# Half-precision parts in the projections of layer A of a two-layer streaming encoder

## The chip, the cores and the metric

The kernel runs on one core of a Trainium2 chip. The metric is the device time of one execution in microseconds (us); the figure for a kernel is the median of its runs. The profile is of one further execution. Its engines are PE (TensorE; its weight loads are shown as PEld), DVE (VectorE), ACT (ScalarE), POOL (GpSimd) and SP (SyncE, which issues all DMAs of this kernel).

## What is computed

There are 2048 prompt tokens and 64 sample tokens of width 1024, and two layers of gated attention with 16 heads of 64. Both layers have the form `x + W_out(attention(RMSNorm(x)) * silu(gate))`; queries, keys, values and gate come from one input projection, and queries and keys are normalised by head.

- Layer A: 16 query heads over 2 key/value heads, a window of a chunk of 64 tokens and the two chunks before, a sink for each head and a bias by relative position.
- Layer B: 16 heads with keys and values of their own, a window of nine chunks, and another bias.

```python
def project(x, norm_g, w_in, q_g, k_g, n_heads, n_kv):
    h = rms_norm(x, norm_g)
    p = h @ w_in
    wq = n_heads * HEAD_DIM
    wkv = n_kv * HEAD_DIM
    q, k, v, gate = jnp.split(p, [wq, wq + wkv, wq + 2 * wkv], axis=-1)
    ...
```

`rms_norm` divides each token by the root of its mean square and multiplies each column by a gain `g`. The kernel puts that gain into the weights.

## The kernel before

**Products of two parts.** All products are of single precision. Each operand is split into a high and a low part, and a product is three matmuls: high by high, high by low, low by high (`project`, lines 796 to 798; the sample unit has both parts of its 64 tokens side by side and needs two, lines 791 and 792). In layer A the parts are of the type fp32r, four bytes wide; in layer B they are float16. Float16 has a narrow range, so layer B brings its operands into range first: weights are multiplied by a power of two found from their largest value, tokens by their row's norm, and the product is multiplied by one constant at its evacuation.

**Units and passes.** Tokens are worked on in units of 256, two tiles of 128, with the 64 sample tokens as a unit of their own. The order is units 0 to 6, the sample, unit 7. Layer A goes over all units four times (passes, `qd` 0 to 3). A pass projects 512 columns, 256 of queries and 256 of gate (four heads); the first pass projects 256 columns of keys and values besides. Then come layer A's output projection, layer B in eight passes over the heads, and its output projection.

**The order of the work.** TensorE's instructions stand in the order in which the program writes them; those of the other engines are placed by a scheduler with a model of the time. A `Filler` holds the projections as generators with costs, and the pipeline of attention items draws on it: attention for tile i runs while the projection is three tiles ahead (`pipeline`). `Filler.step` asks for the next unit's tokens (`prefetch`) when a unit's projection begins, and for the next pass's weights one unit ahead, in passes three and four three units ahead. A `Background` queue holds the splits and evacuations; it is drained in shares between the attention's steps, one or two weight chunks a share, and what a matmul needs is run by force ahead of it (`weights_of`).

**Tokens.** `load_act` loads a unit in four chunks of 128 x 512 into `xraw` (four buffers), casts the high part on ACT (L677), and subtracts on POOL for the low part (L678). The parts are kept in DRAM (`xsa`): units 0 and 1 are split in the first and again in the second pass and stored in the second, the others are split and stored in the first. Later passes load them. `KEEP` holds in which pass a unit is stored. In layer A four loads of 512 KB bring a unit back; in layer B, where the parts are float16, it is two.

**Row norms.** The tokens' factors `rr[0]` come from `row_scales`: it loads the tokens by rows into `xraw`, squares them on ACT with a sum (L772), and raises the mean to -1/2 on POOL (L779). For units 0 and 1 they come from column sums. In layer A the factor of each token is applied when a projection is evacuated (`evacuate`, `evacuate_a`); in layer B `token_rows` spreads the factors over the partitions by a small matmul (L752) and the tokens are multiplied on DVE ahead of the split (L674).

**Weights.** `load_weights` loads chunks of 128 x 512 through three `wraw` buffers. The first set of layer A has twelve chunks (four of keys and values, eight of queries and gate) and later sets have eight. A chunk's high part is made on ACT (L579), its low part on DVE (L582). The loading of a chunk is asked for when the third chunk ahead of it is split.

**Scans.** The scales of layer A's output projection need the largest absolute value of its weights and of the gate's weights. `scan` loads a chunk of 128 x 512 into one buffer and takes a maximum on DVE (L181); `scales_ahead` does so for 16 chunks, every second item from item 20 on, and takes 32 maxima of 128 x 256 from the gate's columns of the split weights (`gate_top`, L261). At items 56 to 58 the scale is worked out (`first_top`, `first_across`, `first_scales`).

**PSUM.** The projections share two banks (`pj`), and attention in layer A has four (`sa`). Line 819 and lines 835 and 836 are evacuations of projections on ACT; line 890 is the multiplication by the head norm on DVE, the last reader of a query/gate bank.

## Time and profile before

| | us |
|---|---|
| median of three runs | 2062.57 |
| lowest, highest | 2062.24, 2062.81 |
| the profiled execution's own time | 2071.44 |
| its span, first to last instruction | 2069.7 |
| granted TensorE clock, mean | 0.992 |

In the profile the projections of layer A lie in these stretches, read from the first and last matmul of 512 columns of each pass: the first from 17.4 to 217.6 us (key/value matmuls start at 6.7), the second from 219.4 to 357.5, the third from 357.8 to 503.2, the fourth from 503.5 to 642.6. The first float16 projection of layer B starts at 841.4.

How to read the rows: a group's row has the line of the program, engine and operation, the tile written and those read, the shape, the count, then busy time and the mean in ns of one, and the engine's idle time just before with what ended it. Matmuls are pipelined and their ends are modelled, so their durations overlap; the distance of their starts tells what one costs. A line can be a helper's. Waits are put down to the releaser that came last.

### The profile page before, as it was taken

What the parts mean: (1) busy time and instruction counts of PE and PEld (TensorE: products, weight loads), DVE (VectorE), ACT (ScalarE), POOL (GpSimd) and SP (SyncE); (2) the same over time, 40 slices, a digit from 0 to 9 for tenths busy, and PEclk for the clock granted to TensorE, in tenths of its full rate; (3) what the DMA queues carried; (4) which work ended last, traced back from release to release, by engine and by line L of the source; (5) the groups of instructions that cost most, each with busy time, mean ns of one, the idle gap of its engine ahead of it and who ended that gap; (6) DMA issues with size and microseconds to landing.
All of it is one profiled execution on the core that took longest, in us unless ns stands there. A gap on an engine that the chain in (4) does not pass through costs nothing.

```text
span 2069.7 us, 40501 instructions
## 1 busy us (share of the span) xinstructions
PE 1975.7 (95%) x12723; PEld 1382.1 (67%) x12723; DVE 1440.7 (70%) x4163; ACT 1438.7 (70%) x3560; POOL 1134.8 (55%) x1529
## 2 busy tenths in 40 slices
PE   7899999999999999989999999999999999999999
PEld 6777777777877888545555555555555555557788
DVE  7666877877778433677667676676767767677673
ACT  6887888777789443377677787786877778687330
POOL 5665565544446323477556575665656656565540
PEclk9999999999999999999999999999999999999999
DMA  8878887998776555698989788897997978698753
GB/s 264 260 210 233 230 215 207 238 243 243 206 187 192 168 177 162 229 235 219 237 177 237 177 201 220 168 253 162 212 211 182 215 167 187 151 189 205 189 158 106
DMA packets 593816, 420.20 MB, mean 203 GB/s; under 512 B 403696, under 2 KB 522880, under 8 KB 593568
## 3 DMA queue, kind: packets, MB, share of 16 engines
q1 hardware_dynamic: 593600, 417.60, 79.9%
q8 instruction: 101, 1.65, 0.3%
q14 instruction: 115, 0.94, 0.1%
HBM read 248.68 MB, written 73.43 MB: 156 GB/s over the span
## 4 chain that ended last, share of the span: by engine, by line
PE 58%; DVE 12%; DMA 10%; ACT 8%; issue 6%; POOL 5%; SPq 1%; POOLq 0%; ACTq 0%; DVEq 0%
PE pj L796 11%; PE pj L798 10%; PE pj L797 10%; PE o L1908 4%; DMA pt<-values 3%; PE sb L1744 2%; PE pj L2164 2%; PE sb L1745 2%; PE pj L2166 2%; PE pj L2165 2%; PE tp L1054 2%; PE pj L2413 2%; PE pj L2417 2%; PE pj L2416 2%; DVE p L1748 1%
## 5 line engine op out<-in xcount | busy, mean ns | idle before, releaser
L796 PE MATMUL pj<-wh,xx 128*128 128x512 f16 (+2 forms) x1648 | 642.9, 390 | 19.8 <-ACT pa L819 9.1
L798 PE MATMUL pj<-wh,xx 128*128 128x512 f16 (+2 forms) x1648 | 624.6, 379 | 0.0
L1801 POOL TENSOR_TENSOR values<-p,values 128x640 f16<-128x640 f32 (+4 forms) x256 | 328.2, 1282 | 206.9 <-ACT values L1800 202.7
L797 PE MATMUL pj<-wh,xx 128*128 128x512 f16 x1024 | 389.9, 381 | 1.3 <-DVE wh L582 1.3
L1760 ACT ACTIVATE p<-p,nm 128x640 f32<-128x640 f32 (+5 forms) x264 | 199.6, 756 | 181.4 <-DVE nm L1753 148.7
L1748 DVE CUSTOM_DVE_ANT_0 p<-sb,BT 128x640 f32<-128x640 f32 (+5 forms) x272 | 196.4, 722 | 148.1 <-PE sb L1745 120.9
L797 PE MATMUL pj<-wl,xx 128*128 128x512 f32 (+1 forms) x624 | 234.8, 376 | 2.3 <-DVE wl L582 2.3
L887 POOL TENSOR_TENSOR f<-f,mhalf 128x4 f32<-128x4 f32 x182 | 188.0, 1033 | 11.7
L798 PEld LDWEIGHTS <-xx 128*128 128x128 f16 x1024 | 100.6, 98 | 123.6 <-issue 3.8
L1561 POOL TENSOR_TENSOR o<-gt,o 128x256 f32<-128x256 f32 (+1 forms) x132 | 106.4, 806 | 139.5 <-ACT p L1391 63.9
L1800 ACT CAST values<-p 128x640 f16<-128x640 f32 (+4 forms) x256 | 168.2, 657 | 12.7 <-DMA pt<-values 6.5
L1391 ACT ACTIVATE p<-p,nm 128x257 f32<-128x257 f32 (+2 forms) x272 | 134.3, 496 | 59.3 <-DVE nm L1380 26.6
L797 PEld LDWEIGHTS <-xx 128*128 128x128 f16 x1024 | 100.6, 98 | 84.2 <-issue 4.9
L796 PEld LDWEIGHTS <-xx 128*128 128x128 f16 x1024 | 100.6, 98 | 82.0 <-issue 1.9
L1908 PEld LDWEIGHTS <-values 128*128 128x128 f16 x1344 | 123.8, 98 | 41.2 <-issue 2.8
L1908 PE MATMUL o<-pt,values 128*128 128x256 f16 (+1 forms) x1344 | 144.7, 256 | 3.6 <-DMA pt<-values 3.6
L796 PEld LDWEIGHTS pj<-wh,xx 128*128 128x128 f32 x624 | 118.6, 190 | 40.3 <-ACT pa L819 11.0
L798 PEld LDWEIGHTS pj<-wh,xx 128*128 128x128 f32 x624 | 118.4, 190 | 23.1
L886 POOL TENSOR_TENSOR f<-f,small 128x4 f32<-128x4 f32 x182 | 38.5, 211 | 172.5 <-DVE f L883 152.7
L797 PEld LDWEIGHTS pj<-wl,xx 128*128 128x128 f32 x624 | 119.1, 191 | 17.6 <-DVE wl L582 3.2
L1556 ACT COPY o<-o 64x256 f32<-64x256 f32 (+1 forms) x264 | 96.1, 364 | 37.8 <-PE o L1908 27.3
L678 POOL TENSOR_TENSOR xx<-xraw,xx 128x512 fp32r<-128x512 f32 (+3 forms) x80 | 97.4, 1233 | 44.3 <-ACT xx L677 44.0
(389 smaller groups left out, 5157.7 us busy)
## 6 DMA issues: line engine op xcount, KB each, us to landing
xx<-xsb SPq DMA_DIRECT2D x112, 512.0 KB, 4.3
xx<-xsa SPq DMA_DIRECT2D x88, 512.0 KB, 5.0
xsa<-xx SPq DMA_DIRECT2D x32, 512.0 KB, 4.2
wl<-in_w_in_b_dram SPq DMA_DIRECT2D x64, 256.0 KB, 4.8
wraw<-in_w_in_b_dram SPq DMA_DIRECT2D x56, 256.0 KB, 3.6
xraw<-in_x_dram SPq DMA_DIRECT2D x40, 256.0 KB, 4.4
xraw<-oga SPq DMA_DIRECT2D x32, 264.0 KB, 3.2
xraw<-ogb SPq DMA_DIRECT2D x32, 264.0 KB, 3.5
```

The costliest lines, as they stand in the source:

```text
L678: nc.gpsimd.tensor_tensor(lo, rv, wide(hi), op=ALU.subtract)
L796: nc.tensor.matmul(ps[:n, :C], xh, wh, start=k == 0, stop=False)
L797: nc.tensor.matmul(ps[:n, :C], xh, wl, start=False, stop=False)
L798: nc.tensor.matmul(ps[:n, :C], xl, wh, start=False, stop=k == KC - 1)
L887: nc.gpsimd.tensor_tensor(fv, fv, mhalf[:n, :H], op=ALU.pow)
L1391: ex = nc.scalar.activation(pv[:n, h % 2, : nk + 1], pv[:n, h % 2, : nk + 1], AF.Exp, scale=-1.0, bias=nm[:n, h : h + 1], accum_out=sm[:n, ...
L1561: nc.gpsimd.tensor_tensor(o1v, gtv, o1v, op=ALU.mult)
L1748: mi = nc.vector.tensor_tensor_reduce(out=p[r, :nk], in0=S[r, o : o + nk], in1=b, op0=ALU.add, op1=ALU.min, scale=1.0, scalar=3e38, accum_ ...
L1760: ex = nc.scalar.activation(p[:n, :nk], p[:n, :nk], AF.Exp, scale=-1.0, bias=it.nm[:n, c : c + 1], accum_out=it.sm[:n, c : c + 1],)
L1800: hi = nc.scalar.copy(two[:, :, 0, :], pv)
L1801: lo = nc.gpsimd.tensor_tensor(two[:, :, 1, :], pv, two[:, :, 0, :], op=ALU.subtract)
L1908: nc.tensor.matmul(it.O[:, h * T + q0 : h * T + q1_], held["VH"][:, kt, h], x, start=kt == kb and not low, stop=kt == tb and low == 1,)
```

## The change

- The first three units of the first pass (`SW = 3`) are projected as before. From the fourth on (`place >= SW`) and in all later passes the projections use float16 parts of tokens that are multiplied by their factor first (`token_rows(unit, 0)`), and weights with a scale (`gsa`); the evacuation multiplies by one constant `C_A(q)`.
- The first pass's weights are therefore split twice: in fp32r for three units, and again in float16. For the second split all twelve chunks are loaded anew, through three raw buffers. Eight are asked for after the last projection of the second unit, four in the third unit after its keys and values, which are now projected for both tiles first. Their scale comes from maxima of the fp32r high parts (`hi_top`, `key_top`), taken between the projections of the second unit's first tile, with a transpose on TensorE in its second tile (`input_across_a`) and a broadcast after it (`input_scales_a`).
- The weights of passes two to four are scanned ahead: 24 scans more, from item -2 on, one for each item up to item 37, where the 16 of the output weights now follow without a pause. `gate_top` is gone; the maxima of whole chunks stand in for it.
- The third unit, too, is split in the first and again in the second pass (`KEEP`), and `xsa` is float16: two transfers of 512 KB for a unit in place of four.
- Of the multiplications by the row factors, those of every second chunk go to POOL, the others to DVE.
- Row norms from the fifth unit on are worked out two units ahead of the one being projected instead of one.
- The second pass's weights are asked for two units ahead, half of them first.

```diff
+SW = 3
+KEEP = [1] * SW + [0] * (NU + 1 - SW)
...
     def scan_source(i):
+        if i >= 100:
+            return w_qg_a[(i - 92) // 8, (i - 100) % 8 // 2, :, i % 2, :]
...
+    def hi_top(w, i, ks, part):
         for k in ks:
             wt, j = w[k]
             r = nc.vector.tensor_reduce(
+                most[:, i + k : i + k + 1], wide(wt.h[:, j, part]), axis=AX.X, op=ALU.max,
                 apply_absolute_value=True,
             )
+            behind(r.ins, bg.anchors.get(r.ins.engine, held["ms"]))
...
+    def input_across_a(q):
+        ps = psum_a("sa", 512, 4)
+        nc.tensor.transpose(ps[0:1, 0:P], top[:, 15 + q : 16 + q], ident)
+        m, e, r = (row[:, i : i + 1] for i in (60, 61, 62))
+        nc.vector.tensor_reduce(m, ps[0:1, 0:P], axis=AX.X, op=ALU.max)
+        nc.vector.tensor_scalar(m, m, 1e-12, 1.0, op0=ALU.max, op1=ALU.mult)
+        powers(m, e, r)
+        times(row[:, 46:47], r, WB_)
+        times(row[:, 47:48], e, 1 / (HB * WB_))
+
+    def input_scales_a(q):
+        ps = psum_a("sa", 512, 4)
+        nc.tensor.matmul(
+            ps[:, 0:2], ones[0:1, 0:1].to_broadcast([1, P]), row[:, 46:48], start=True, stop=True
+        )
+        nc.vector.tensor_copy(scl[:, 10 + q, 0:2], ps[:, 0:2])
+        times(gsa[:, q], gain[:, 0, :], scl[:, 10 + q, 0:1])
+        held["known", q] = True
...
+    xs = [dr.tile([P, 2 * KC * TOK], dt, tag=n, name=n) for n, dt in (("xsa", F16), ("xsb", F16))]
...
+        def place_first(i):
+            tag = ("wx", "ws", "wh")[i // 4]
+            return t(tag, [P, 1024], WN if i >= 8 else 4, F16)
...
                     if rows is not None:
-                        (nc.vector).tensor_tensor(
+                        (nc.gpsimd if cache is xs[0] and c % 2 == 0 else nc.vector).tensor_tensor(
...
+                if half_parts:
+                    assert ("known", qd) in held
+                    rows = None if qd > KEEP[u] else token_rows(unit, 0)
+                    st.x[qd, u] = x = load_act(
+                        x0, u * UT, T, False, T == TS, None, cache, qd > KEEP[u], F16, rows
+                    )
+                else:
+                    st.x[qd, u] = x = load_act(x0, u * UT, T, sums, T == TS, lead)
...
                 if qd not in st.emit:
-                    (st.w[qd],), _, st.emit[qd] = load_weights(0, (w_qg_a[qd], 512))
+                    assert ("known", qd) in held
+                    (st.w[qd],), _, st.emit[qd] = load_weights(1, (w_qg_a[qd], 512), scale=gsa[:, qd])
...
+                    if qd == 0 and place >= SW - 1:
+                        for later in order[place + 2 + (it is not mine[0]) : place + 3 + (it is not mine[0])]:
+                            if later[0] not in held["normed"]:
+                                row_scales(later)
+                                held["normed"].add(later[0])
+                    if qd == 0 and place == SW - 1:
+                        if it is mine[0]:
+                            for it2 in mine:
+                                out = []
+                                c = yield from project(it2.tile, xc, st.wkv, 256, out)
+                                take_kv(it2, out[0])
+                                yield c
+                            st.emit_more(4)
...
+                    if qd == 0 and u == 1:
+                        if it is mine[0]:
+                            key_top(st.wkv)
+                            hi_top(st.w[0], 24, range(8), slice(0, 512))
+                        else:
+                            input_top_a(0)
+                            input_across_a(0)
                     out = []
                     c = yield from project(it.tile, xc, st.w[qd], 512, out)
                     take_qg(it, out[0])
+                    if qd == 0 and u == 1 and it is mine[1]:
+                        input_scales_a(0)
+                        st.halves, _, st.emit_more = load_weights(
+                            1, (w_qg_a[0], 512), (w_kv_a, 256), scale=gsa[:, 0], apart=None
+                        )
+                        st.emit_more(8)
...
-            filler.add(prefetch, weights if place == 0 else None, first if qd == 0 and u == 0 else gen, 3 * (qd > 1))
+            filler.add(prefetch, weights if place == 0 else None, first if qd == 0 and u == 0 else gen, (0, 2, 3, 3)[qd])
...
         def scales_ahead(i):
+            n = i + 2
+            if 0 <= n < 40:
+                scan(100 + n if n < 24 else 60 + n)
+            elif n == 40:
                 scan()
...
+            if i == 42:
                 first_top()
+            elif i == 44:
                 first_across()
+            elif i == 46:
                 first_scales()
```

123 lines of the change are left out of this document (64 added, 59 removed).

## The prediction, made before the result was known

> **What bounds the kernel now.** I read the page first, then a table of windows cut at the passes of layer A, then the waits of TensorE in those windows, then the groups by shape, and last single matmuls in order of time.
>
> ```profile
> span 2069.7 us, 40501 instructions
> PE 1975.7 (95%) x12723; PEld 1382.1 (67%) x12723; DVE 1440.7 (70%) x4163; ACT 1438.7 (70%) x3560; POOL 1134.8 (55%) x1529
> ```
>
> The page says only that TensorE is busy nearly all the time. Whether a faster matmul shortens the kernel has to be read in the stage that is changed. The columns below are the window, its length, then the busy time of PE, PEld, DVE, ACT and POOL, the granted clock, the DMA share and GB/s. The rows are: the first pass around its fourth unit, the rest of the first pass, and passes two, three and four.
>
> ```profile
> 37.00:90.00 53.00, 44.21 (x267) 37.00 (x267) 39.10 (x128) 43.63 (x125) 33.59 (x53) 0.97 0.92 281
> 90.00:219.00 129.00, 119.68 (x755) 100.73 (x756) 87.30 (x304) 102.59 (x279) 74.26 (x109) 0.99 0.80 222
> 219.00:358.00 139.00, 137.15 (x792) 109.99 (x791) 104.90 (x342) 116.94 (x318) 80.05 (x133) 1.00 0.81 216
> 358.00:503.00 145.00, 139.07 (x797) 110.98 (x796) 111.44 (x345) 110.88 (x311) 70.55 (x126) 0.99 0.93 239
> 503.00:643.00 140.00, 137.00 (x790) 110.17 (x788) 107.45 (x352) 114.68 (x313) 73.42 (x123) 1.00 0.79 210
> ```
>
> These are two different stages. In passes two to four (219 to 643, 424 us) TensorE idles 1.9, 5.9 and 3.0 us; ACT, the next engine, is at 84%, 76% and 82%. TensorE sets the pace there. In the first pass it idles 8.8 of 53 us and 9.3 of 129. Who ends those waits (us in total, times, longest), first in 219 to 643, then in 90 to 219:
>
> ```profile
> PE o L1452 <- DMA pt<-values: 5.5, 4, 2.4
> ```
> ```profile
> PE pj L796 <- ACT pa L819: 7.1, 3, 3.1
> PE pj L796 <- DVE pa L890: 2.8, 3, 1.2
> ```
>
> In the later passes half of the idle time is a transposing DMA that lands late. In the first pass the query/gate projection of a tile waits for the evacuations of what was projected before it: a chain over ACT and DVE, and TensorE is ahead of it.
>
> **The matmuls.** The change turns the operands of most projections of layer A from fp32r into f16. Both types are in the trace with the same shape (busy us, mean ns), layer B's as f16 and layer A's as f32:
>
> ```profile
> L797 PE MATMUL pj<-wh,xx 128*128 128x512 f16 x1024 | 389.9, 381 | 1.3 <-DVE wh L582 1.3
> L798 PE MATMUL pj<-wh,xx 128*128 128x512 f16 x1024 | 389.6, 380 | 0.0
> L798 PE MATMUL pj<-wh,xx 128*128 128x512 f32 x512 | 203.8, 398 | 0.0
> L797 PE MATMUL pj<-wl,xx 128*128 128x512 f32 x512 | 203.7, 398 | 2.3 <-DVE wl L582 2.3
> ```
>
> The means differ by 17 to 18 ns. Durations overlap in the pipeline, so I check by start times: the first four below are layer A's, and the last four layer B's.
>
> ```profile
> 300.17 0.39 PE L796 MATMUL pj<-wh,xx 128*128 128x512 f32 x1
> 300.40 0.39 PE L797 MATMUL pj<-wl,xx 128*128 128x512 f32 x1
> 300.62 0.39 PE L798 MATMUL pj<-wh,xx 128*128 128x512 f32 x1
> 300.86 0.39 PE L796 MATMUL pj<-wh,xx 128*128 128x512 f32 x1
> ```
> ```profile
> 870.37 0.66 PE L752 MATMUL tp<-ident,rms 128*128 128x128 f32 x4
> 870.87 0.38 PE L796 MATMUL pj<-wh,xx 128*128 128x512 f16 x1
> 871.09 0.38 PE L797 MATMUL pj<-wh,xx 128*128 128x512 f16 x1
> 871.30 0.38 PE L798 MATMUL pj<-wh,xx 128*128 128x512 f16 x1
> 871.52 0.38 PE L796 MATMUL pj<-wh,xx 128*128 128x512 f16 x1
> ```
>
> Three steps take 0.69 us in fp32r and 0.65 in f16, at the same granted clock: 13 ns a matmul with the rounding of the rows, 17 by the means; I take 17. Is it the type, or the stage? Rows of one stage, 128x256 of either type, decide it:
>
> ```profile
> 56.77 0.36 PE L796 MATMUL pj<-wh,xx 128*128 128x256 f32 x1
> 56.98 0.28 PE L797 MATMUL pj<-wl,xx 128*128 128x256 f32 x1
> 57.09 0.28 PE L798 MATMUL pj<-wh,xx 128*128 128x256 f32 x1
> 57.21 0.28 PE L796 MATMUL pj<-wh,xx 128*128 128x256 f32 x1
> ```
> ```profile
> 311.14 0.27 PE L1369 MATMUL sa<-KA,q 128*128 128x256 f16 x1
> 311.25 0.27 PE L1370 MATMUL sa<-KA,q 128*128 128x256 f16 x1
> ```
>
> From 56.98 to 57.21 two fp32r matmuls take 0.115 us each; layer A's own f16 scores follow at 0.11. At half the width the difference is about half, as for a cost by the column.
>
> The Trainium skill, "TensorE: Matmul & The Clock Gate", section "Back-to-back issue gap", gives N / 2.4 + 2.5 ns between matmuls of N columns, 216 ns at 512, and under "Weight-path perf modes" says that the array takes one element per cell and cycle whatever the element's width. The f16 rows (0.216 us) agree, and the fp32r rows (0.23) do not. By that rule alone the term below would be 0 and the sum +10.1 us.
>
> So many are converted: in the first pass five full units of two tiles and the sample unit, and in passes two to four 48 full tiles and three samples. A full tile has 24 matmuls of 512 columns, a sample 16: 58 x 24 + 4 x 16 = 1456, by 17 ns = **-24.8 us**; 4.4 of it lies in the first pass, 20.4 in the other three. All of it is on the path in the latter, by the idle times above. In the first pass the saving of a query/gate projection counts too, since the chain that the next one waits for starts at its end. The key/value projections (256 matmuls by some 8 ns, 2 us) end in front of that wait: I count **0**, bounds 0 and -2.
>
> **What is added to TensorE.** Token rows: 17 tiles, one 128-column matmul each; the four of L752 take 0.50 us together, so 17 x 0.125 = **+2.1 us**, 1.4 of it in the first pass. The transposes and broadcasts of the four new scales are a few tenths.
>
> **The hand-over in the first pass.** Between the second unit's projection and the fourth unit's, the kernel takes maxima of the first weights, works out a scale, and loads and splits twelve weight chunks once more. The rows for it, and for the other edits on ACT and DVE:
>
> ```profile
> L579 ACT ACTIVATE wh<-wraw,gain 128x512 fp32r<-128x512 f32 x28 | 19.8, 717 | 5.3 <-DMA wraw<-in_w_qg_a_dram 4.9 <-PE pj L798 0.2
> L582 DVE SCALAR_TENSOR_TENSOR wl<-wraw,gain,wh 128x512 fp32r<-128x512 f32 x28 | 22.7, 823 | 3.3 <-ACT wh L579 3.2
> L582 DVE SCALAR_TENSOR_TENSOR wh<-wl,gsb,wh 128x512 f16<-128x512 f32 x64 | 63.5, 1011 | 4.1 <-ACT wh L579 4.1
> L181 DVE TENSOR_REDUCE most<-scan 128x1 f32<-128x512 f32 x24 | 16.2, 676 | 8.1 <-DMA scan<-in_w_in_b_dram 8.1
> L261 DVE TENSOR_REDUCE most<-wh 128x1 f32<-128x256 f32 x32 | 11.9, 409 | 0.0
> L674 DVE TENSOR_TENSOR xraw<-xraw,rows 128x512 f32<-128x512 f32 x32 | 26.4, 867 | 1.4 <-DMA xraw<-x 1.1
> L772 ACT ACTIVATE res<-xraw 128x512 f32<-128x512 f32 x26 | 16.3, 627 | 8.8 <-DMA xraw<-in_x_rows_dram 8.8
> ```
>
> On ACT, between 37 and 90 us: 12 x 0.72 = 8.6, and one unit's row squares that move ahead, 4 x 0.63 = 2.5; together 11.1. ACT is free for 53.0 - 43.6 = 9.4. On DVE: eight maxima at 0.68 and four at 0.41 (7.1), twelve low parts at 0.82 to 1.01 (11), four products with the token rows at 0.87 (3.5) and four scans (2.7), less eight of the old gate maxima at 0.41 (3.3): 21. DVE is free for 53.0 - 39.1 = 13.9. So 7 us do not fit on DVE and 2 on ACT. TensorE will show it in places where it waits in order: the new transpose of the maxima, the token-rows matmul of the fourth unit, and that unit's first key/value matmul. Behind each stand the projection and the scores of the tiles in the pipeline. For the second place a row gives a size, the row norms of the fourth unit:
>
> ```profile
> 57.84 0.70 POOL L779 TENSOR_TENSOR rms<-ms,mhalf 128x2 f32<-128x2 f32 x1 [0.28 <-DVE ms L778]
> ```
>
> They are there at 58.5, while TensorE would reach the matmul when the third unit's work starts, before 56.77: some 2 us of waiting, within the 7. I take **+7 us**. The lower bound is 0, if DVE's backlog falls on work that nothing waits for. The upper bound is the serial sum of ACT's and DVE's additions, 11 + 21 = 32.
>
> The row loads that move ahead pass the third and fourth units' x loads on SP's queue, and draw on the same four raw buffers; they have a unit of lead more than before, so I count nothing beyond the above. The twelve weight loads pass through three raw buffers; SP issues in order, so an attention tile's transpose or output store may wait behind one of them. An x load that comes late, or a store behind such a wait, is inside the upper bound.
>
> **The steady cost.** The other scans and products are 0.7 to 2 us a tile on DVE and POOL, which have a quarter of their time free. In the second pass the third unit is now split instead of loaded: four more passes of ACT over 512 columns, 2.5 us by the row of L772. ACT there goes from 84% of 139 us to (116.9 + 2.5) / 132, some 90%. A tighter engine lets TensorE wait now and then; idle time in 219 to 643 is 10.8 us now, and I add **+3 us** (bounds 0, and 10, half of those passes' gain).
>
> **The transfers.** The kept parts are half as wide.
>
> ```profile
> xx<-xsa SPq DMA_DIRECT2D x88, 512.0 KB, 5.0
> xsa<-xx SPq DMA_DIRECT2D x32, 512.0 KB, 4.2
> ```
>
> Some 60 MB become 30; twenty-four scans, twelve weight chunks and one unit read twice give back some 10 MB. None is on the path itself, but the late transposing DMA (5.5 us) stands in the same queue, in the pass with a DMA share of 0.93: **-2 us**, bounds 0 and -5.5.
>
> **The sum.** -24.8 + 0 + 2.1 + 7 + 3 - 2 = -14.7 us. The profiled execution took 2071.4 us (span 2069.7) and would take 2056.7; the median of the runs shown is 9 us lower, so the same sum gives 2062.6 - 14.7 = 2048 us.
>
> **The rivals.** *All of it fits*: DVE's backlog is hidden, the key/value gain counts and the transposing DMA is never late. -24.8 - 2 + 2.1 - 5.5 = -30: 2033 us. For it speaks that ACT and DVE have free time in every window; against it the 21 us of work in 13.9.
> *ACT takes the pace*: half of the later passes' gain is lost, +10 in place of +3, and the DMA gives nothing back: -24.8 + 2.1 + 7 + 10 = -5.7: 2057 us. For it speaks ACT's 90% in the second pass; against it that TensorE idles only 1.9 us there at 84%.
> *The hand-over runs in series* (slower): weights come through three buffers, each split waits for ACT, then DVE, and the fourth unit's first matmul waits for all. It costs 32 instead of 7: -24.8 + 2.1 + 32 + 3 - 2 = +10: 2073 us. It decides from 22 us on. Against it: the splits are spread over the third unit's two tiles, some 24 us, and hold only matmuls of the fourth.
> *The type costs nothing* (slower): the distance belongs to the stage, and only costs remain, +10.1: 2073 us. The 256-column rows speak against it.
>
> **How the numbers follow.** The forecast has 0.62, all fits 0.15, ACT takes the pace 0.13, the series 0.06, no gain by type 0.04. About 0.2% (4.1 us) is what a measurement can tell from no change. The forecast, all fits and half of the ACT case are faster by more: 0.83; the other half is the same: 0.07; the two last are slower: 0.10. The range, 2035 to 2060, holds the forecast with its bounds, the ACT case and most of the first rival.
>
> **What would show it.** Matmuls of 512 columns on lines 796 to 798 in layer A at 381 ns and 0.216 us apart; the three later passes down from 424 us to about 405; the first pass ending some 4 us later than 219, with a wait of TensorE between 45 and 90 us for DVE or ACT; the transposing DMA's wait below 5.5. Wrong would be: fp32r's spacing in f16 rows, TensorE idle by over 20 us between the passes' ends, or a single wait of over 20 us at the fourth unit.

## The result, and the profile after

The changed kernel takes 2096.19 us (median of 4, 2092.41 to 2099.12) against 2062.69 for the kernel before beside it: a ratio of 1.0152, interval 1.0124 to 1.0181. The change is slower by 33.5 us in the medians (31 us by the ratio), and the forecast of 2048 us was wrong in sign. The profiled execution took 2092.41 us.

The page of the changed kernel opens so:

```profile
span 2090.6 us, 40588 instructions
PE 1968.0 (94%) x12769; PEld 1273.9 (61%) x12769; DVE 1497.9 (72%) x4251; ACT 1448.5 (69%) x3580; POOL 1157.3 (55%) x1551
```

TensorE's busy time fell by 7.7 us and VectorE's grew by 57.2. The windows view, cut where the four passes of layer A end (the columns are those of the prediction's table):

```profile
0.00:246.60 246.60, 198.01 (x1173) 141.28 (x1174) 209.79 (x595) 179.38 (x466) 150.61 (x206) 0.92 0.78 227
246.60:391.70 145.10, 137.04 (x815) 83.50 (x813) 113.14 (x364) 116.03 (x316) 84.62 (x137) 0.96 0.65 170
391.70:542.90 151.20, 137.95 (x804) 81.99 (x803) 111.25 (x350) 112.53 (x314) 69.76 (x126) 0.95 0.66 167
542.90:674.20 131.30, 128.44 (x784) 78.11 (x781) 100.91 (x331) 113.16 (x312) 71.82 (x122) 1.00 0.51 130
```

The four passes of the kernel before, cut likewise, took 217.6, 139.9, 145.7 and 139.4 us at a granted clock of 0.98, 1.00, 0.99 and 1.00. The first of them:

```profile
0.00:217.60 217.60, 188.50 (x1141) 158.03 (x1141) 154.11 (x513) 168.00 (x444) 128.57 (x187) 0.98 0.82 239
```

So the first pass is 29 us longer, the second and third over 5 each, and only the fourth gains, 8 us. In the first pass VectorE (the third engine column) is busy for 209.8 us where it was for 154.1, and the clock column (the first after POOL) drops from 0.98 to 0.92. To see what that does, I split TensorE's time in layer A into work counted at full clock, idle time, and half of the time that it was busy at half clock (worked out from the records of matmuls and of the clock):

| layer A, us | before | after | difference |
|---|---|---|---|
| TensorE's work at full clock | 597.7 | 574.7 | -23.0 |
| TensorE idle | 39.9 | 72.8 | +32.9 |
| lost to half clock | 5.1 | 26.6 | +21.5 |
| end of the fourth pass | 642.6 | 674.0 | +31.4 |

The rest of the kernel is layer A's output projection and layer B, which the change does not edit; it was 10.5 us shorter in this profile than in that of before, and varies by as much between the profiles of all kernels here.

**Each matmul gained what was forecast.** Starts in the fourth pass, by the timeline:

```profile
599.74 0.38 PE L841 MATMUL pj<-wh,xx 128*128 128x512 f16 x1
599.96 0.38 PE L842 MATMUL pj<-wh,xx 128*128 128x512 f16 x1
600.17 0.38 PE L840 MATMUL pj<-wh,xx 128*128 128x512 f16 x1
600.39 0.38 PE L841 MATMUL pj<-wh,xx 128*128 128x512 f16 x1
```

They stand 0.216 us apart. The DMA share of the second and third pass fell from 0.81 and 0.93 to 0.65 and 0.66; kept parts move as

```profile
xx<-xsa SPq DMA_DIRECT2D x42, 512.0 KB, 4.1
xsa<-xx SPq DMA_DIRECT2D x16, 512.0 KB, 4.7
```

about half as many as before. What ate both gains is in TensorE's waits, first from 37 us to the end of the first pass, then in the three others (total, times, longest):

```profile
PE tp L1096 <- DVE ms L822: 7.0, 1, 7.0
PE tp L1096 <- DVE pa L1003: 5.1, 1, 5.1
PE pj L840 <- DVE pa L932: 4.9, 3, 3.2
PE pj L841 <- DVE wh L636: 4.8, 3, 2.5
```
```profile
PE o L1529 <- DVE pl L1062: 7.7, 8, 2.3
PE o L1529 <- DMA pt<-values: 3.4, 2, 3.1
PE tp L1096 <- DVE sm L1485: 2.9, 1, 2.9
PE tp L217 <- DVE q L1407: 2.9, 1, 2.9
```

Nearly all of them are VectorE: 33.9 us of 37.4 in the first of these stretches, where the kernel before had 9.7 of 18.8. The longest, 7.0 us, falls in the hand-over. VectorE's timeline there:

```profile
81.20 0.29 DVE L1003 TENSOR_TENSOR pa<-pa,f 128x128 f32<-128x128 f32 x1
...
82.34 0.75 DVE L636 SCALAR_TENSOR_TENSOR ws<-wraw,gsb,ws 128x512 f16<-128x512 f32 x1
...
85.09 0.74 DVE L636 SCALAR_TENSOR_TENSOR ws<-wraw,gsb,ws 128x512 f16<-128x512 f32 x1
...
87.28 0.67 DVE L185 TENSOR_REDUCE most<-scan 128x1 f32<-128x512 f32 x1
87.87 0.47 DVE L932 SCALAR_TENSOR_TENSOR pa<-pj,rms,f 128x256 f32<-128x256 f32 x1
```

There is hardly a gap from 81.2 to 88.3. The evacuation at 87.87, for which TensorE's transposes wait, stands in order behind attention, low parts of the second split and a scan. (The profile names the small operation right behind it.)

**The second wait is a VectorE operation stretched beside GpSimd.** The same view of GpSimd and VectorE near the end of the first pass:

```profile
227.06 0.60 POOL L1487 TENSOR_TENSOR G<-pb,sm 128x256 f32<-128x256 f32 x1
227.63 1.26 POOL L720 TENSOR_TENSOR xraw<-xraw,rows 128x512 f32<-128x512 f32 x1
228.86 0.69 POOL L990 TENSOR_TENSOR f<-f,mhalf 128x2 f32<-128x2 f32 x1
229.53 1.14 POOL L1483 TENSOR_TENSOR values<-p,values 128x512 f16<-128x512 f32 x1
230.64 3.36 POOL L724 TENSOR_TENSOR xx<-xraw,xx 128x512 f16<-128x512 f32 x3
```
```profile
227.00 7.28 DVE L1003 TENSOR_TENSOR pa<-pa,f 64x256 f32<-64x256 f32 x1 [0.55 <-POOL f L990]
234.21 0.67 DVE L1062 TENSOR_TENSOR pl<-sa,ph 128x512 f16<-128x512 f32 x1
```

One VectorE operation takes 7.28 us, from the start of an unbroken run of seven GpSimd operations until 0.3 us after its end; the sixteen of the line in this pass with twice the partitions and half the columns take 0.56 on the mean. It is the extreme of something common. If each VectorE operation of the first pass is set against the shortest of its kind, 26.0 us of stretching in the kernel before became 49.1. The Trainium skill, "SBUF — State Buffer", section "Who interferes with whom", says that a VectorE instruction with two SBUF inputs contends with a GpSimd instruction that reads SBUF. The rows agree. That such an instruction can lose to several GpSimd instructions in a row is read from these times; no view names what holds an operation within its own duration.

**Idle time was paid twice.** Windows of 3.4 us in the first pass, cut on the grid on which the granted clock changes:

```profile
112.20:115.60 3.40, 2.81 (x26) 2.34 (x24) 2.96 (x10) 3.34 (x11) 1.21 (x2) 1.00 1.02 332
115.60:119.00 3.40, 1.16 (x6) 0.60 (x7) 2.11 (x8) 2.71 (x10) 1.06 (x2) 1.00 0.92 268
119.00:122.40 3.40, 3.40 (x10) 1.27 (x9) 2.86 (x9) 2.59 (x9) 2.74 (x5) 0.50 0.55 170
122.40:125.80 3.40, 3.40 (x22) 2.04 (x21) 1.12 (x5) 2.22 (x6) 0.85 (x2) 1.00 0.91 231
```

TensorE idles for 2.24 us of the second window, and the whole third is granted half the clock: 10 matmuls in place of 22. Over the twenty traces of this study, a window at full clock with under 1.2 us of idle time was followed by one at half clock 0 times in 11180, with 1.2 to 1.6 us once in 219, with 1.6 to 2.0 us 34 times in 178, with more 198 times in 201. So a wait of over 2 us within a window costs up to 1.7 us more. The Trainium skill, "TensorE: Matmul & The Clock Gate", section "HAM oscillation — how this bites in real kernels", warns of TensorE gaps over some 3.4 us; the windows here lose their clock at 2.

### The profile page after: what moved, and what is told of

It reads as the page before. It is cut to its first block, busy times and chain, and to the rows that moved or that the text cites. A ratio compares the mean times of both kernels' runs of the same rounds, so it can differ in the third digit from the quotient of the medians.

```text
span 2090.6 us, 40588 instructions
## 1 busy us (share of the span) xinstructions
PE 1968.0 (94%) x12769; PEld 1273.9 (61%) x12769; DVE 1497.9 (72%) x4251; ACT 1448.5 (69%) x3580; POOL 1157.3 (55%) x1551
## 4 chain that ended last, share of the span: by engine, by line
PE 52%; DVE 18%; ACT 10%; DMA 8%; issue 7%; POOL 5%; SPq 1%; ACTq 0%; POOLq 0%; DVEq 0%
PE pj L840 9%; PE pj L841 9%; PE pj L842 9%; PE o L1987 4%; PE pj L2243 2%; PE pj L2245 2%; PE pj L2244 2%; PE sb L1823 2%; PE sb L1824 2%; DVE p L1457 2%; DMA pt<-values 2%; PE tp L1096 2%; PE pj L2492 2%; PE pj L2496 2%; PE pj L2495 2%
## 5 line engine op out<-in xcount | busy, mean ns | idle before, releaser
L840 PE MATMUL pj<-wh,xx 128*128 128x512 f16 (+3 forms) x1568 | 590.2, 376 | 8.7 <-DVE values L897 2.3
L842 PE MATMUL pj<-wh,xx 128*128 128x512 f16 (+3 forms) x1568 | 586.9, 374 | 0.6 <-POOL xx L724 0.6
L841 PE MATMUL pj<-wh,xx 128*128 128x512 f16 (+1 forms) x1488 | 558.6, 375 | 5.3 <-DVE wh L636 5.3
L842 PEld LDWEIGHTS <-xx 128*128 128x128 f16 x1568 | 154.6, 99 | 187.4 <-issue 12.3
L840 PEld LDWEIGHTS <-xx 128*128 128x128 f16 x1568 | 154.6, 99 | 138.1 <-issue 16.3
L841 PEld LDWEIGHTS <-xx 128*128 128x128 f16 x1568 | 154.7, 99 | 123.2 <-issue 7.7
L929 POOL TENSOR_TENSOR f<-f,mhalf 128x4 f32<-128x4 f32 x182 | 186.8, 1026 | 11.9
L932 DVE SCALAR_TENSOR_TENSOR pa<-pj,scl,f 128x256 f32<-128x256 f32 x178 | 85.4, 480 | 54.8 <-POOL f L929 52.8
L1457 DVE CUSTOM_DVE_ANT_0 p<-sa,BT,nsink 128x256 f32<-128x256 f32 (+2 forms) x272 | 116.4, 468 | 11.4 <-PE sa L1447 6.5
L724 POOL TENSOR_TENSOR xx<-xraw,xx 128x512 f16<-128x512 f32 (+2 forms) x84 | 98.7, 1194 | 40.0 <-ACT xx L723 40.0
L1639 DVE TENSOR_TENSOR o<-o,o 64x256 f32<-64x256 f32 (+1 forms) x264 | 108.3, 410 | 11.3 <-ACT o L1635 8.9
L1407 DVE SCALAR_TENSOR_TENSOR q<-tp,qf,q 64x256 f16<-64x256 f32 x128 | 61.7, 482 | 54.3 <-ACT gt L1625 36.9
```

Source lines behind the costliest of these rows:

```text
L840: nc.tensor.matmul(ps[:n, :C], xh, wh, start=k == 0, stop=False)
L841: nc.tensor.matmul(ps[:n, :C], xh, wl, start=False, stop=False)
L842: nc.tensor.matmul(ps[:n, :C], xl, wh, start=False, stop=k == KC - 1)
L929: nc.gpsimd.tensor_tensor(fv, fv, mhalf[:n, :H], op=ALU.pow)
L1457: mi = nc.vector.tensor_tensor_reduce(out=pv[:n, h % 2, :nk], in0=Sv[h][:n, :nk], in1=bias[h][:n, b0 : b0 + nk], op0=ALU.add, op1=ALU.min, ...
L1639: nc.vector.tensor_tensor(o1v[rows], Ov[0:64, :, hh, :], o1v[rows], op=ALU.add)
```

## The experiments

**The theory** after the two traces: TensorE's gain is real, but the first pass is set by a chain over ScalarE, VectorE and GpSimd; the products ahead of the casts and the scans lengthen it, and waits of over 2 us take the clock as well. **The rivals**: the hand-over alone costs it; the clock reacts to the half-precision matmuls; the products cost nothing and the loads do it. "Before" stands for the kernel before, run beside each.

**Taking parts out of the change.** The first kernel multiplies by the row's factor at the evacuation (`factor(tt)`: the row norm by `C_A`, one small GpSimd operation a tile), so that raw tokens are split and there are no products; the second has the scales as constants, with no scans of input weights, no maxima and no scale chains; the third has both. A constant scale, here and below, leaves out working it out from the weights.

```diff
-                        x0, u * UT, T, False, T == TS, None, cache, qd > KEEP[u], F16, rows
+                        x0, u * UT, T, False, T == TS, None, cache, qd > KEEP[u], F16, None
...
-                it.kv = pr = evacuate(C_A(0) if half_parts else rr[0][:, tt : tt + 1], n, ps, 256, 0)
+                it.kv = pr = evacuate(factor(tt), n, ps, 256, 0)
```
```diff
+    nc.vector.memset(scl[:, 10:14, 0:1], 4096.0)
...
-            if 0 <= n < 40:
-                scan(100 + n if n < 24 else 60 + n)
+            if 24 <= n < 40:
+                scan(60 + n)
```

> The changed kernel with float16 parts of the tokens as they are: no token rows on TensorE and none of the 36 products with them on DVE and POOL; the factor of a token goes into the evacuation, as in the kernel before. Theory (DVE sets the pace in the first pass, and each idle stretch of TensorE of over 2 us is followed by 3.4 or 6.8 us at half clock): DVE loses some 21 us of work, the first pass ends 10 to 20 us earlier than 246.5, half-clock time in layer A falls from 68 to below 45 us, and the time is 2070 to 2085. Rival 1 (float16 matmuls themselves bring the clock down): no change in half-clock time, 2090 to 2096. Rival 2 (only the place of the hand-over matters, its second split and its in-order waits): 2088 to 2096.

> The changed kernel with one fixed power of two as scale of all input weights of layer A: the 24 scans, the 12 maxima of the first weights and the four chains of small instructions for the scales are left out (it holds only for weights in the range of these); second split and products stay. Theory: DVE loses 24 x 0.68 + 7 = 23 us of work, 12 of it in the first pass, and the transposes at which TensorE waited; 2072 to 2086. Rival 1 (clock by float16): 2090 to 2096. Rival 2 (hand-over alone): the second split stays, so 2085 to 2092.

> Both of the two before together; the second split of the first weights is what is left of the hand-over. Theory: DVE has 44 us less work, the first pass comes back to within 10 us of the kernel before, passes two to four keep their 20 us: 2050 to 2065. Rival 1: 2090 to 2096. Rival 2: 2080 to 2090.

| layer A, us | time, ratio to before (interval) | passes 1 to 4 | idle | lost to half clock |
|---|---|---|---|---|
| the change | 2096.2, 1.0152 (1.0124 to 1.0181) | 246.5, 145.1, 151.2, 131.3 | 72.8 | 26.6 |
| no products | 2080.4, 1.0077 (1.0047 to 1.0108) | 233.4, 134.4, 148.2, 132.8 | 62.1 | 16.1 |
| constant scales | 2085.6, 1.0094 (1.0069 to 1.0119) | 236.9, 140.6, 151.1, 132.4 | 69.2 | 18.8 |
| both | 2063.9, 0.9990 (0.9974 to 1.0006) | 221.5, 132.7, 149.0, 132.8 | 54.5 | 11.4 |

Products (with their token rows) cost 16 us, or 22 where the scales are constant; scans, maxima and scale chains 11, or 17 without products; both together 32. By the ratios these are 15, 21, 12, 18 and 33 us. Within the intervals that is the whole loss. (The second kernel's time lies in the range of the theory and in that of the hand-over; the two others lie in the theory's alone.) All of the hand-over stands in the kernel without products, which is faster by 16 us, so the hand-over alone isn't the loss; the third kernel keeps of it only the second split, and breaks even, so the second split alone isn't it either. (Each ratio is to runs of before on the same chip; their median went from 2062.7 to 2067.7 between chips, so a difference of a few us between two chips is read from the ratios. The passes are those of one profile each: a later edit, to the third pass alone, left a first pass 3.4 us longer, so differences of 3 us between passes tell nothing.)

The third kernel missed in one thing: its passes two to four were to keep their 20 us, and they are 10.5 us shorter than in the kernel before, 414.5 us in place of 425.0.

**Taking out the hand-over as well.** Constant scales and raw tokens from the first unit on: no second split, and 34 us less work for TensorE in layer A than in the kernel before.

```diff
-SW = 3
-KEEP = [1] * SW + [0] * (NU + 1 - SW)
+SW = 0
+KEEP = [1, 1] + [0] * (NU - 1)
```

> Float16 from the first unit on, raw tokens and a fixed scale: no second split, no scans of the input weights, no products. What is left is the type of the operands and half the traffic of the kept parts. Theory: the gain of the matmuls, 24.8 us and 4 more for the first three units, comes out nearly whole: 2030 to 2042, with half-clock time in layer A not above the 10 us of the kernel before. Rival 1 (clock by float16): half-clock time stays above 50 us, 2070 or more. Rival 2: as the theory, 2030 to 2042; it differs from the theory in the two first runs.

Measured 2065.8 us, 0.9998 (0.9982 to 1.0013). The expectation missed. Its first three passes:

```profile
0.00:219.60 219.60, 181.12 (x1141) 116.59 (x1142) 150.29 (x510) 166.67 (x442) 130.09 (x223) 0.95 0.79 223
219.60:356.10 136.50, 130.83 (x800) 79.58 (x799) 103.84 (x337) 118.03 (x320) 82.42 (x151) 1.00 0.63 163
356.10:506.40 150.30, 138.00 (x804) 82.76 (x803) 111.21 (x347) 111.75 (x313) 73.32 (x143) 0.95 0.67 167
```

TensorE has 172.2 us of work in the first pass in place of 185.1, and the pass takes 219.6 in place of 217.6: idle 38.5 us instead of 29.1, and 8.8 lost to half clock instead of 3.4. TensorE doesn't set the first pass, so no gain of TensorE shows there. The later passes are the greater part of the miss: they took 419.4 us in place of 425.0, a gain of 5.6 us of the 20 forecast. The second and fourth gained 3.4 and 6.8 us, but the third got 4.6 us longer: TensorE idles 12.3 us in it instead of 5.9, and 6.0 are lost to half clock. The stretch to layer B was 6 us longer as well. So even without products, scans and hand-over most of the gain isn't on the path.

**Two small edits on the third kernel.** The first adds eight unread matmuls ahead of a unit's projection in the first pass, to keep the clock up; the second gives the small transposes of the output scales a scores bank, since TensorE waited 2.9 us in the third pass for the one bank that a VectorE operation (`q`, line 1407) still read; the third has both.

```diff
+                    if qd == 0 and place >= SW and it is mine[0] and not heads_up:
+                        spare_ps = psum("o", 512, 1)
...
+                        for e in range(8):
+                            nc.tensor.matmul(spare_ps, xc.parts[0][0][:, 0, 0:P], wf, start=True, stop=True)
```
```diff
-        ps = tp_bank()
+        ps = tp_bank() if a != 12 else psum_a("sa", 512, 4)
```

> Raw tokens and fixed scales as before (2063.9), and ahead of the query/gate projection of the first tile of five units of the first pass TensorE does eight matmuls of 512 columns whose results nobody reads: 8 x 0.216 = 1.7 us of work at the places where it idles 2 to 3.6 us. Theory (a window of 3.4 us with 2 us or more of idle time is followed by half clock): the idle time falls below 2 us there, half-clock time in the first pass from 17 to 10 us or less, and the time falls by 3 to 8 us, 2056 to 2061. Rival (the clock follows something else, such as float16's power): half-clock time stays, and 5 x 1.7 us are added where nothing was waited for, 2064 to 2072.

> Raw tokens and fixed scales as before (2063.9), with the transposes and the broadcast for the scale of layer A's output projection in a bank of the scores in place of the one bank that the transposes of queries share, which DVE still reads when they come (waits of 2.9 and 1.1 us in the third pass). Theory: these waits go, and the half clock after the first of them: 4 to 6 us off the third pass, 2057 to 2061. Rival (TensorE then waits for the same DVE work one instruction later): 2063 to 2065.

> The two edits together, on raw tokens and fixed scales: the spare matmuls and the other bank. Theory: 8 to 14 us below 2063.9, 2050 to 2056, faster than the kernel before. Rival (clock by something else): 2061 to 2070.

The unread matmuls: 2068.5 us, 1.0016 (1.0005 to 1.0026), first pass 232.3. They had to wait for their own bank, 7.2 us in all, and only made the loop longer: this says nothing on the clock. The bank: 2062.0, 0.9977 (0.9961 to 0.9993), between its two expectations, third pass 145.2 after 149.0; by a little the fastest of the study, but with constant scales. Both: 2063.0, 0.9984 (0.9970 to 0.9999), a miss.

**The costs alone, on the kernel before**, in fp32r and without a hand-over: products by ones from the fourth unit on, half on GpSimd and half on VectorE, and the twenty-four scans at the change's density, results unused; then each alone. These kernels keep the 32 maxima of the gate's weights (11.9 us of VectorE), which the change drops, so they load VectorE by more than the change does.

```diff
+    unit_rows = t("rows", [P, UT], 1)
+    nc.vector.memset(unit_rows, 1.0)
...
-                        (nc.vector).tensor_tensor(
+                        (nc.gpsimd if cache is xs[0] and c % 2 == 0 else nc.vector).tensor_tensor(
```
```diff
-            if 20 <= i < 52 and i % 2 == 0:
-                scan(84 + (i - 20) // 2)
+            n = i + 2
+            if 0 <= n < 40:
+                scan(200 + n if n < 24 else 60 + n)
```

> The kernel before, all of layer A in fp32r, with the work that the change gives to DVE and POOL ahead: 24 more scans of layer A's input weights, one for each item from -2 on, and products with a row of ones in the six units of the first pass from the fourth on and the two that are split in the second, every second one on POOL. No float16, no second split. Theory (DVE's load sets the pace of the first pass): the first pass gets 8 to 18 us longer, with more half-clock time; 2074 to 2088. Rivals (clock by float16; hand-over alone): within 5 us of the kernel before, 2061 to 2071.

> The kernel before, unchanged in type, scale and order, plus one thing: the four element-wise products of a unit's raw rows (here by ones, so that the values stay), half on VectorE and half on GpSimd, from the fourth unit of the first pass on. Theory (VectorE's and GpSimd's added work sets the first pass, and each idle stretch of 2 us in a clock window costs a half-clock window behind it): about half of the 33 us of products and scans together, so 2076 to 2086 us; the first pass ends at 222 to 230 us, VectorE is busy 8 to 12 us more in it, TensorE's work at full clock in it stays within 2 us of 185, and idle and half-clock loss together rise by 5 to 13 us there. Rival (the products hide, the scans do all of it): 2062 to 2070. Rival (the products alone do it, since each one makes GpSimd and VectorE stretch each other): over 2090.

> The kernel before plus one thing: twenty-four scans of the later passes' weights (a load of 256 KB and a maximum on VectorE each), at one per attention item from the first, as the change has them, with the sixteen old ones behind them at the same density; their results are not used. Theory: the other half of the 33 us, 2074 to 2084 us; the first pass ends at 222 to 228, VectorE 8 to 12 us more in it, work unchanged. With the products' run the two differences add to 33 within 8 us. Rival (scans hide): 2062 to 2070. Rival (the scans' 6 MB of loads, not their maxima, do it): the same total, but TensorE's waits behind DMAs grow, not those behind VectorE.

Both: 2099.3 us, 1.0158 (1.0143 to 1.0174), above the expected range. Products alone: 2088.4, 1.0102 (1.0078 to 1.0125), a little over its expectation. Scans alone: 2079.9, 1.0062 (1.0041 to 1.0083). The differences, 20.7 and 12.2, add to the 33.4 of both. With both, layer A loses 12.9 us to half clock instead of 5.1, in fp32r throughout, so the clock doesn't react to the type. But the way of the scans differs. VectorE's maxima in layer A (busy, mean | idle before them), with the scans alone and in the change:

```profile
L183 DVE TENSOR_REDUCE most<-scan 128x1 f32<-128x512 f32 x42 | 28.4, 676 | 16.1 <-DMA scan<-in_w_o_a_dram 15.4 <-DMA scan<-in_w_qg_a_dram 0.7
```
```profile
L185 DVE TENSOR_REDUCE most<-scan 128x1 f32<-128x512 f32 x40 | 26.8, 671 | 3.1 <-DMA scan<-in_w_o_a_dram 3.1
```

With fp32r's traffic, VectorE stands 16.1 us at the head of its queue for scans that have not landed. In the change, with half of that traffic, it stands 3.1. The like sizes are in part a coincidence, and the weight lies on the first table, not on this sum.

**Which engine's product costs.** The products of the kernel before put all on VectorE, all on GpSimd, and on VectorE beside the chain (on a constant tile, so that no split waits for them); then the change itself with all on GpSimd, and all on VectorE. The edit is that of one line:

```diff
-                        (nc.gpsimd if cache is xs[0] and c % 2 == 0 else nc.vector).tensor_tensor(
+                        (nc.gpsimd if cache is xs[0] else nc.vector).tensor_tensor(
...
+                        nc.vector.tensor_tensor(
```

> As the products' run (the kernel before plus products by ones), but all of them on VectorE and none on GpSimd. It adds some 28 products of 0.87 us, 24 us, to VectorE in the first pass. Theory A (what counts is how long VectorE is busy): worse than the half-and-half run's 2088, 2095 to 2105. Theory B (what counts is that GpSimd, which does the subtraction that ends each split, gets a second operation of 1.3 us in the same chain and slows VectorE beside it): better, 2068 to 2080.

> As the products' run, but all products on GpSimd, which adds some 28 of 1.29 us, 36 us, to it in the first pass and none to VectorE. Theory A: better than half and half, 2070 to 2080. Theory B: worse, 2095 to 2110. If both this and the run with all on VectorE cost about 20 us, it is neither engine's load but the place of the product in the chain from load to split.

> As the run with all products on VectorE, but each product is done on a constant tile (two operations of 256 columns) at the same place in VectorE's queue: the same work for the engine, and the split of the rows waits for none of it. If VectorE's load is what costs, it is within 5 us of the run with all products on VectorE; if the product's place in the chain costs, it is within 6 us of the kernel before, 2062 to 2074.

> The change with all its products on GpSimd instead of every second one. Theory (VectorE's load in the first pass is what delays): VectorE's products, 12 of 1.3 us in the first pass, go, GpSimd gets as many of some 1.4 us; the first pass is 3 to 8 us shorter and the time 2080 to 2092 us. Rival (GpSimd's products slow VectorE's operations with two inputs beside them as much as they relieve it): 2092 to 2100. Rival (GpSimd's chain of products becomes the last thing the projection waits for): over 2100, with TensorE's waits at the projection named GpSimd.

> The change with all its products on VectorE (half and half: 2096 us; all on GpSimd: 2104). If the product's place ahead of the cast costs and an engine's time hardly matters, 2093 to 2101. If VectorE's load decides, over 2101. If GpSimd's products, by stretching VectorE's operations beside them, are the costly ones, below 2093; on the kernel before, all on VectorE cost 16 us, half and half 21, all on GpSimd 21, which speaks for this.

| us | half and half | all on GpSimd | all on VectorE |
|---|---|---|---|
| kernel before with products by ones | 2088.4 | 2086.8, 1.0106 (1.0091 to 1.0122) | 2082.7, 1.0082 (1.0065 to 1.0099) |
| the change | 2096.2 | 2104.2, 1.0182 (1.0161 to 1.0203) | 2084.9, 1.0087 (1.0062 to 1.0112) |

On the kernel before, all three placings cost 16 to 21 us, and neither theory's range held either run. By what the second expectation adds, that points to the product's place between load and split, on either engine; it isn't shown, since each placing also loads the engine that it is on. In the change, moving the products onto VectorE made it faster by 11 us (13 by the ratios, whose intervals lie apart). Moving them off VectorE did not help: 8 us slower in the medians, 6 by the ratios, whose intervals overlap, and in the traces the first pass is not longer (244.9 us against 246.5). So the theory that VectorE's busy time decides falls, at least for the products, and a product on GpSimd is the dear one. Over 2100 us had been expected of TensorE waiting for GpSimd's products, but such waits are 2.6 us; 29.5 us of its waits in the first pass are for VectorE. VectorE's rows of the change and of the change with all products on VectorE, both in the first pass:

```profile
L720 DVE TENSOR_TENSOR xraw<-xraw,rows 128x512 f32<-128x512 f32 x12 | 15.6, 1323 | 0.0
L986 DVE CUSTOM_DVE_ANT_0 sq<-pa 128x64 f32<-128x64 f32 x28 | 9.1, 360 | 2.8 <-ACT pa L862 2.8
```
```profile
L720 DVE TENSOR_TENSOR xraw<-xraw,rows 128x512 f32<-128x512 f32 x24 | 18.4, 809 | 0.6 <-DMA xraw<-in_x_dram 0.6
L986 DVE CUSTOM_DVE_ANT_0 sq<-pa 128x64 f32<-128x64 f32 x28 | 8.3, 332 | 0.9 <-ACT pa L862 0.9
```

and of the change with all on GpSimd:

```profile
L986 DVE CUSTOM_DVE_ANT_0 sq<-pa 128x64 f32<-128x64 f32 x28 | 17.8, 671 | 5.1 <-ACT pa L862 5.1
```

Twice the products take VectorE only 2.8 us longer when no product of GpSimd runs beside them (809 ns instead of 1323), and the key norms' squares go from 332 to 671 ns when all do. VectorE's stretching in the first pass is 33.5 us with all on VectorE, 49.1 with half, 42.5 with none. So it sets the run with all on VectorE apart from the two others, but not these from each other.

The products beside the chain took 2073.9 us, 1.0054 (1.0030 to 1.0079), but its six runs fall in two groups, four from 2072.0 to 2074.9 and two from 2082.0 to 2083.5, and since they waited for nothing they ran between 36.7 and 83.6 us and not over the whole pass. It doesn't tell VectorE's load from the place in the chain.

**Later scans, and a later start.** The kernel before with the extra scans from the second pass on; the third kernel with the bank and half precision only from the second pass on; and the change without products, with its true scales, the bank, and ten instead of eighteen scans in the first pass.

```diff
+            if 17 <= i < 57:
+                old = i % 2 == 0 and 20 <= i < 52
+                scan(84 + (i - 20) // 2 if old else 200 + extra[0])
```
```diff
-SW = 3
+SW = 99
```
```diff
+            if 0 <= n < 8:
+                scan(100 + n)
...
+            elif 15 <= i < 23:
+                scan(108 + i - 15)
```

> As the run with twenty-four scans, one per attention item as there, but the extra ones start with the second pass instead of the first. Theory (scans cost where a chain over ScalarE and VectorE sets the pace, and little where TensorE does): the first pass ends at 217 to 219 us again, the later passes lose 0 to 4 us, 2064 to 2071. Rival (a scan costs some 0.5 us wherever it stands): 2077 to 2083.

> Half precision only from the second pass on: the first pass is all fp32r as in the kernel before, the second pass splits every unit again in half precision on raw rows with one fixed weight scale (no token rows, no products, no extra scans or maxima; valid for these inputs), passes three and four load kept half-precision parts; the small transposes of the output scales use a scores bank. Theory (the first pass does not gain from the type and is best left alone; only passes without element-wise work can take the gain): first pass within 4 us of the kernel before's 218, second pass 138 to 146 us because ScalarE has four more units to split, passes three and four 6 to 8 us shorter each; 2048 to 2060 us. Rival (the gain of passes two to four is lost to ScalarE's tighter second pass): 2062 or more.

> The change with the row factor at the evacuation in place of the products (as in the run without products, 2080 us), the true scales kept, the twenty-four scans spread (ten instead of eighteen in the first pass, the others one per item from the second pass on, where half precision has brought the DMA share down to 0.65 and a scan's load should land in time), and the output scales' small transposes in a scores bank. Theory (VectorE's load in the first pass costs; behind it TensorE sets the pace): the first pass 4 to 8 us shorter than the 233 of the run without products, the third pass some 3 us shorter by the bank, 2068 to 2076 us. Rival (a scan costs the same anywhere, as the run with later scans on the kernel before suggests): 2077 to 2082.

The later scans: 2087.6 us, 1.0102 (1.0078 to 1.0127), worse than scans from the start. The first pass ends at 218.4 again, but the third takes 160.2 us in place of 145.7 and the fourth 144.9. The expectation missed both ways, and the row says why:

```profile
L183 DVE TENSOR_REDUCE most<-scan 128x1 f32<-128x512 f32 x41 | 27.9, 681 | 37.6 <-DMA scan<-in_w_o_a_dram 21.0 <-DMA scan<-in_w_qg_a_dram 16.6
```

In the passes whose DMA share was 0.79 to 0.93, a scan lands late, and VectorE stands 37.6 us in front of such loads while TensorE's evacuations queue behind.

Half precision from the second pass on: 2075.6, 1.0029 (1.0011 to 1.0048), a miss; the passes took 223.3, 146.3, 145.5 and 132.0. Splitting every unit again costs the second pass what its matmuls gain (idle 12.9 us), and the first pass lost 9.9 us to half clock with idle time as before (29.9): a few waits came over the 2 us.

The spread scans: 2075.9, 1.0048 (1.0031 to 1.0066), at the upper edge of its expectation; without spreading and bank, 2080.4. The first pass went from 233.4 to 231.0, less than the 4 to 8 us expected, the third from 148.2 to 141.8, of which the bank may be some 4. Here the scans' loads are in time, with 1.7 us of VectorE's idle time before 43 maxima:

```profile
L185 DVE TENSOR_REDUCE most<-scan 128x1 f32<-128x512 f32 x43 | 29.0, 675 | 1.7 <-DMA scan<-in_w_o_a_dram 1.7
```

## Why the prediction was wrong, point by point

- **What bounds the kernel**: right as read of the kernel before (TensorE in passes two to four, a chain over ScalarE and VectorE in the first), and then not used. If a chain sets the first pass, whatever is put into the chain counts in full and TensorE's saving counts for nothing there; the kernel without a hand-over shows both.
- **The matmuls**, -24.8, and **token rows**, +2.1: -22.7 forecast, -23.0 measured as work at full clock. 17 ns a matmul holds, though the 256-column rows (0.115 against 0.11 us) were thin ground for it. But the work saved is not time saved. Of the -4.4 booked in the first pass nothing was gained. Of the -20.4 of the later passes, "All of it is on the path" was a second step that failed: without products, scans and hand-over 5.6 us came out, with the second split 10.5, and with the other bank besides 15.7. The idle times of the kernel before did not tell what waits there once TensorE is faster; in the third pass TensorE then idles 11 to 13 us in place of 5.9.
- **The key/value projections at 0**: nothing of the first pass's saving showed, these included. That fits the reason given, which no run tests by itself.
- **The hand-over**, +7: the fourth unit's first projection started at 103.3 us instead of 90.4, so 12.9. The longest wait (7.0 us) is for VectorE's backlog, as the step had it, though at none of the three places named. Without products that projection still starts at 102.9, with constant scales at 100.8, and only without both at 93.0. Behind it the first pass lost another 16.0 us, which the step did not have.
- **The steady cost**, +3, is the step that failed. "The other scans and products are 0.7 to 2 us a tile on DVE and POOL, which have a quarter of their time free": taken out of the change, with the hand-over's own maxima and products, the two are worth 32 us. Between the traces of the change and of the kernel without both, layer A differs by 38 us: 10.3 up to the fourth unit's first projection, in the hand-over, then 14.7 in the rest of the first pass, and 12.4, 2.2 and -1.5 in the passes behind it. So what was put at 3, with 10 as its bound, is some 28 us in these traces. Three things were left out. The products stand ahead of every cast, in the chain that sets the first pass, and ScalarE's casts wait for them:

```profile
L723 ACT CAST xx<-xraw 128x512 f16<-128x512 f32 x32 | 18.9, 614 | 13.2 <-DVE xraw L720 8.1 <-POOL xraw L720 5.0
```

  How much of the loss this is stays open: with all products on GpSimd the casts idle for 1.5 us in place of 13.2, and the kernel is no faster. The price of 0.87 us was of layer B, where no product of GpSimd runs beside it; here it is 1.32, and other operations of VectorE stretch with it. And VectorE and GpSimd work in order (the timeline at 81 to 88 us shows it for VectorE), so that an evacuation behind a scan or a product waits even in an engine with free time on average. Which of the three weighs most the runs do not part.
- **Idle time at its own length**: a second omission. Of the 54.4 us by which idle and half clock grew, 21.5 are half clock. The page of before had such windows, and I didn't look at what precedes them.
- **The transfers**, -2: the transposing DMA's wait fell from 5.5 to 3.4 us. Right, and small.
- **The rivals**: "ACT takes the pace" named the kind of thing and the wrong engine. "The hand-over runs in series" gave 2073 and the right sign, by a mechanism that isn't this one: no wait was over 7.0 us. "The type costs nothing" gave 2073 too, and the spacing of 0.216 us refutes it. Of the signs named for a wrong forecast one came: TensorE idle for 24.2 us between the ends of the first and the fourth pass.

Left open: why the stretch from the last projection of layer A to layer B is some 2 to 6 us longer in several of the kernels; how much of a product's cost on the kernel before is its place in the chain and how much VectorE's load; and why the third pass idles more with half-precision parts even where no product and no extra scan is left.

## What to carry to other kernels

An average share of free time doesn't say that an operation fits: ask whether it stands in the chain that sets its stage, what is queued behind it in order, and which engine it slows while it runs. A faster matmul is worth something only in a stage that TensorE sets; the first step is to take the gain alone, without its price, and see whether the time moves. Price an operation by a row with the same neighbours, and add up to 1.7 us to the price of a wait of TensorE of over 2 us.

## What the runs showed of the hardware

- The granted clock goes by a fixed grid of 3.41 us: more than 2.0 us of TensorE idle time in one window took half the clock from the next in 198 of 201 cases. In the first 650 us alone it was 42 of 42 in the kernels whose layer A is all fp32r, and 88 of 88 in the others.
- A VectorE operation with two inputs in SBUF takes longer beside GpSimd operations: 7.28 us in the worst case, beside seven in a row, and 0.81 against 1.32 us for the same product without and with products on GpSimd beside it.
- Matmuls of 512 columns of the same stage, layer A, are 0.23 us apart in fp32r before and 0.216 in f16 after.
